# Down projection: the two sums of weight blocks per row block, made by GpSimd, are made by VectorE

## The chip, the cores and the metric

The kernel runs on one core of one Trainium2 chip. A core has a TensorE (PE in the profile: matmuls; PEld: its weight loads), a VectorE (DVE), a ScalarE (ACT), a GpSimd (POOL) and a SyncE (SP), which here only issues DMAs. Each engine works through a queue of its own, in order, and they meet at semaphores. The metric is the device time of one execution in microseconds (us). Kernel before: 2428.02 us, the median of 3 runs (2427.6 to 2429.95).

## The reference

One layer of a hybrid streaming encoder for 512 prompt frames and 64 sample frames: attention in two head groups, an output projection, and then the part this change is in, a gated feed-forward network with a residual:

```python
x = x + mix @ lp['w_out']
h = rmsnorm(x, lp['norm_ffn_g'])
x = x + (jax.nn.silu(h @ lp['ffn_w_gate']) * (h @ lp['ffn_w_up'])) @ lp['ffn_w_down']
```

The model width is 2048, the inner width of the network 5632, all in float32, so `ffn_w_down` is 5632 x 2048. A final RMSNorm closes the computation.

## The kernel before

Every product of two float32 matrices is split: an operand `w` becomes `wh`, its rounded high part (made by ScalarE, `split` at L156), and `wl`, the rest `w - wh` (made by VectorE, L153). Three matmuls, `wh*xh`, `wh*xl` and `wl*xh`, then stand for one product.

Gate, up and down projections use a seven-product scheme for 2 x 2 blocks (`winograd`). A weight tile of 256 input rows by 256 columns is taken as four 128 x 128 blocks, a11, a12, a21, a22, and the token side as two halves of 288 tokens each. Products 1, 2 and 4 take a11, a12 and a22 as they are; the others take sums, which the kernel makes on the way:

```text
product 5: s5 = a21 + a22    (GpSimd)      product 3: s3 = a12 - s6   (VectorE)
product 6: s6 = s5 - a11     (VectorE)     product 7: s7 = a11 - a21  (GpSimd)
```

Line L1192 makes all four of them. One statement picks the engine: GpSimd for products 5 and 7, VectorE for 6 and 3.

The down projection goes over the 44 input blocks of 128 in five blocks of 4 pairs and a last one of 2 pairs. For each of the first five and for each of 8 pairs of output blocks, `down_rows` runs `winograd` once; that is 40 calls, which the text below calls *row blocks*. A row block loads 1 MB of weights (`raw`, 128 x 8 x 256), and its sums are 128 x 512. For each of the seven products, in the order 1, 5, 6, 2, 7, 3, 4 (`CHAIN`), TensorE runs 8 matmuls with `wh` (L1206) and 4 with `wl` (L1210), each of 288 columns. Then VectorE adds the product from PSUM into the residual `y` (L1472). The products of a chain share PSUM banks: 1, 6, 7 and 4 use bank a, 5 and 3 bank b.

What sets the order of the work: each engine's queue is written by a scheduler, which puts an instruction where its operands and buffers allow it. Three pools of buffers matter. `wh` and `wl` have two buffers each. The sums `ws` have three (one in the first row block, where some are made in place), so that a sum takes the place of an earlier one that the split of that one has just read. `raw` has two buffers from the third row block on: the load for row block r+2 is issued on SP's queue when the last split of row block r (the `wl` of product 4) has read its tile. The operands `b` of the token side were stored to memory by the gate and up projections; those of the next block are loaded, on the same queue of SP, while the present block is computed.

The last block of 2 pairs is not done by `winograd` but by plain matmuls (`plain_rows`, L189), and the final norm and the transposes of the result close the kernel.

Of the kernel before, what the change touches and what calls it, by code (L numbers as in the profile page):

```python
# [14 lines left out]
ALU = mybir.AluOpType  # L15
# [30 lines left out]
class Streams:  # L46
# [15 lines left out]
    def take(self, name):  # L62

        free = self.slots[name]
        while not free or free[0] > self.now:
            yield max(free[0] - self.now, 0.01) if free else 0.1
        free.pop(0)
# [48 lines left out]
def encoder_step(  # L116
# [8 lines left out]
    V, S, G = nc.vector, nc.scalar, nc.gpsimd  # L125
# [29 lines left out]
    def split(hi, lo, src):  # L155
        S.activation(hi, src, AF.Copy)  # L156
        sub_lo(lo, src, hi)
# [933 lines left out]
    def pool(name, side="left"):  # L1091
        cm = tc.tile_pool(name=name, bufs=1, side=side, reuse_waits="tile")
        return cm.__enter__(), lambda: cm.__exit__(None, None, None)
# [9 lines left out]
    CHAIN = ((1, "a"), (5, "b"), (6, "a"), (2, "c"), (7, "a"), (3, "b"), (4, "a"))  # L1103
# [10 lines left out]
    def quarters(b1, b2):  # L1114
        return b1[:, 0:QH], b1[:, QH:TQ], b2[:, 0:QH], b2[:, QH:TQ]
# [35 lines left out]
    def pmt():  # L1151
        return pm.tile([P, 512], F32, name="m", tag="m")

    def winograd(wpool, spool, raws, slots, take, banks=None, engine=V, step=lambda: None, stag=("ws", 1),
                 chain=(), made=None, within=True):

        first, last = not banks, take is not None
        banks = {} if banks is None else banks

        def split_weights(n, srcs):
            wh = wpool.tile([P, n, P], F32R, name="wh", tag="wh", bufs=2)
            wl = wpool.tile([P, n, P], F32R, name="wl", tag="wl", bufs=2)
            k = 0
            for s in srcs:
                split(wh[:, k:k + s.shape[1], :], wl[:, k:k + s.shape[1], :], s)  # L1170
                k += s.shape[1]
            return wh, wl

        vs = [r.rearrange("p (m t) (f c) -> p t f m c", t=2, f=2) for r in raws]
        n = sum(v.shape[3] for v in vs)
        a11, a12, a21, a22 = ([v[:, t, f] for v in vs] for f in range(2) for t in range(2))
        sums = []

        def lhs(p):
            if made and p in made:  # L1180
                return made[p]
            if p in (5, 6, 3, 7) and (p == 5 or not within):
                w = spool.tile([P, n, P], F32, name="ws", tag=stag[0], bufs=stag[1])
                ends = np.cumsum([0] + [x.shape[1] for x in a21]).tolist()
                new = [w[:, a:b, :] for a, b in zip(ends, ends[1:])]
            else:
                new = {6: sums, 3: a12, 7: a21}.get(p)
            if p == 5:
                sums.extend(new)
            left, right = {5: (a21, a22), 6: (sums, a11), 3: (a12, sums), 7: (a11, a21)}.get(p, ((), ()))  # L1190
            for x, y, z in zip(new or (), left, right):
                (G if p in (5, 7) else V).tensor_tensor(x, y, z, op=ALU.add if p == 5 else ALU.subtract)  # L1192
            if p == 6:
                sums[:] = new
            return split_weights(n, new or {1: a11, 2: a12, 4: a22}[p])

        shared = {}
        for p, name in chain or [(p, p) for p in ORDER]:
            new = name not in shared
            if first:  # L1200
                shared[name] = banks[p] = shared[name] if not new else pmt()[:, 0:QH]
            wh, wl = lhs(p)
            for k in range(n):
                hi, lo = operands[slots[k], p]
                for x in (hi, lo):
                    PE.matmul(banks[p], wh[:, k, :], x, start=first and new and k == 0 and x is hi, stop=False,  # L1206
                              skip_group_check=not new)
            for k in range(n):
                hi, lo = operands[slots[k], p]
                PE.matmul(banks[p], wl[:, k, :], hi, start=False, stop=last and k == n - 1,  # L1210
                          skip_group_check=not new)
            if last:
                take(p, banks)
            step()
# [10 lines left out]
    ws = {}  # L1225
# [13 lines left out]
    for i in range(KC):  # L1239
        x = ma.tile([P, TQ], F32, name="x", tag="x", bufs=3)  # L1240
# [28 lines left out]
    fw, close_fw = pool("fw")  # L1269

    def load_pair(pool, src, c0, first=0):
        r = pool.tile([P, 16, 256], F32, name="raw", tag="raw", bufs=1)
        for i in range(2 - first):
# [4 lines left out]
    raw = load_pair(fr, w_gate, 0, 1)  # L1278
    banks0 = {}
    winograd(ma, ma, [raw0], range(4), None, banks0, step=lambda: next(turning, None), stag=("wr", WR_BUFS),  # L1280
             made={p: ws[2 * KC + p - 1] for p in (1, 2)})
    close_ma()
# [7 lines left out]
    def combined(c11, c12, c21, c22, chain):  # L1290

        s4 = None if chain else squad()
        s = {}
        copied = {1: c11, 5: c22, 6: c12, 4: c21}
        added = {2: (c11,), 7: (c22,) if chain is CHAIN else (c22, c21), 3: (c12,)}

        def take_sums(p, banks):
            if p in copied:
                S.activation(copied[p], banks[p], AF.Copy)
            else:  # L1300
                for c in added[p]:
                    V.tensor_tensor(c, c, banks[p], op=ALU.add)  # L1302

        if chain:
            return take_sums

        def take(p, banks):
            if p == 1:
                s[1] = s4[:, 0]
                S.activation(s[1], banks[1], AF.Copy)  # L1310
            elif p == 6:
                s[2] = s4[:, 1]
                V.tensor_tensor(s[2], s[1], banks[6], op=ALU.add)
                V.tensor_tensor(c12, s[2], banks[5], op=ALU.add)
            elif p == 3:
                V.tensor_tensor(c12, c12, banks[3], op=ALU.add)
            elif p == 7:
                V.tensor_tensor(s[2], s[2], banks[7], op=ALU.add)
                V.tensor_tensor(c22, s[2], banks[5], op=ALU.add)
                V.tensor_tensor(c21, s[2], banks[4], op=ALU.add)  # L1320
            elif p == 2:
                V.tensor_tensor(c11, s[1], banks[2], op=ALU.add)

        return take
# [47 lines left out]
    y = {}  # L1372
# [14 lines left out]
    for u in range(FC // 2):  # L1387
        out = {}
        for which, wsrc in (("g", w_gate), ("u", w_up)):
# [6 lines left out]
            chain = () if first else CHAIN if u == FC // 2 - 1 and which == "u" else WIDE  # L1396
            take = combined(*quarters(c[:, 0, :], c[:, 1, :]), chain)
# [8 lines left out]
            def step():  # L1406
                products[0] += 1
                if products[0] > (2, 1)[which == "u"]:
                    next(spilling, None)
                if u == 0 and which == "u":  # L1410
                    next(norm, None)
                if u == FC // 2 - 1 and which == "u":
                    if products[0] == 2:
                        load_y(0)
                    for _ in range(blocks[0]):
                        next(start, None)

            if first:
                winograd(fw, rw, [now], range(4, 8), take, banks0, step=step)
            else:  # L1420
                winograd(fw, rw, [now], range(8), take, step=step, chain=chain)
# [43 lines left out]
    def down_rows(m0, n, d, slots, step):  # L1465
        raws = [fetched.pop((m0, d))]
        y11, y12, y21, y22 = quarters(y[2 * d], y[2 * d + 1])
        parts = {1: (y11,), 5: (y22,), 6: (y12,), 2: (y11,), 7: (y22,), 3: (y12,), 4: (y21,)}

        def take(p, banks):  # L1470
            for c in parts[p]:
                V.tensor_tensor(c, c, banks[p], op=ALU.add)  # L1472

        spool, bufs = (yy, 3) if m0 + d else (rw, 1)
        winograd(fw, spool, raws, slots, take, step=step, stag=("ws", bufs), chain=CHAIN, within=m0 + d == 0)

    tok = [[(0, NS), (NS, P), (192, 96)], [(QH, P), (416, P), (544, 32)]]
    sqs = {}
# [72 lines left out]
    wanted, m0 = [], 0  # L1551
# [16 lines left out]
    for bi, n in enumerate(blocks):  # L1568
        slots = [(first + k) % 8 for k in range(n)]
        if bi + 1 < len(blocks):  # L1570
# [7 lines left out]
            for d in range(KC // 2):  # L1578
                if bi == 0 and d + 1 < KC // 2:
                    load_y(d + 1)  # L1580
                down_rows(first, n, d, slots, step)
                fetch_raw()
                if bi + d == 0:
                    for _ in spilling:
                        pass
                    close_rw()
                    yy, close_yy = pool("yy", "right")
# [89 lines left out]
```

## Time and profile before

| what | us |
| --- | --- |
| median of 3 runs | 2428.02 |
| the profiled execution, its own time | 2432.31 |
| its span (first to last instruction) | 2430.4 |
| TensorE busy in the span | 2379.0 |
| VectorE busy | 1895.8 |
| ScalarE busy | 1133.6 |
| GpSimd busy | 768.7 |
| the down projection's row blocks, in the span | 1892 to 2348 |

The profile is of one execution. What lies around its span is 1.9 us. It is read in groups (instructions of one line, engine and tile, with busy time and mean duration), in waits (who waited for whom, total, times, longest), and in the timeline, where each row has a start, a duration, the engine, the line, the tiles written and read, and in brackets the idle time of the engine ahead of it with what ended that. The profile shows tiles without buffer numbers, so that `wl<-ws,wh` may be the split of any of the sums.

### The profile page before, as it was taken

What the parts mean: (1) busy time and instruction counts of PE and PEld (TensorE: products, weight loads), DVE (VectorE), ACT (ScalarE), POOL (GpSimd) and SP (SyncE); (2) the same over time, 40 slices, a digit from 0 to 9 for tenths busy, and PEclk for the clock granted to TensorE, in tenths of its full rate; (3) what the DMA queues carried; (4) which work ended last, traced back from release to release, by engine and by line L of the source; (5) the groups of instructions that cost most, each with busy time, mean ns of one, the idle gap of its engine ahead of it and who ended that gap; (6) DMA issues with size and microseconds to landing.
All of it is one profiled execution on the core that took longest, in us unless ns stands there. A gap on an engine that the chain in (4) does not pass through costs nothing. (4 is left out here: it accounts for less than half of the span.)

```text
span 2430.4 us, 44051 instructions
## 1 busy us (share of the span) xinstructions
PE 2379.0 (98%) x17556; PEld 2342.8 (96%) x17556; DVE 1895.8 (78%) x2748; ACT 1133.6 (47%) x1984; POOL 768.7 (32%) x515
## 2 busy tenths in 40 slices
PE   7999999999999999999999999999999999999998
PEld 6999999989999999999999999999999999999997
DVE  5666676666665688888888888888888899888875
ACT  5455554434444554444445444444444333333355
POOL 1100000020000355465455555554554222222235
PEclk9999999999999999999999999999999999999998
DMA  8533333243333553444454445345446983663434
GB/s 226 140 94 92 85 95 91 76 142 103 104 97 109 172 153 115 153 155 134 145 163 144 138 153 163 128 144 163 146 136 210 316 280 110 228 218 107 129 105 148
DMA packets 363250, 353.02 MB, mean 145 GB/s; under 512 B 25086, under 2 KB 321684, under 8 KB 363044
## 3 DMA queue, kind: packets, MB, share of 16 engines
q1 hardware_dynamic: 361039, 344.48, 44.9%
q0 software_dynamic: 1680, 5.19, 0.7%
q8 instruction: 138, 2.26, 0.4%
q10 hardware_dynamic: 325, 0.53, 0.1%
q14 instruction: 68, 0.56, 0.1%
HBM read 271.68 MB, written 81.16 MB: 145 GB/s over the span
## 5 line engine op out<-in xcount | busy, mean ns | idle before, releaser
L1206 PE MATMUL m<-b,wh 128*128 128x288 f32 x7168 | 1046.0, 295 | 0.9 <-ACT wh L156 0.8
L1206 PEld LDWEIGHTS m<-b,wh 128*128 128x128 f32 x7168 | 982.8, 188 | 1.8 <-ACT wh L156 1.4
L1210 PE MATMUL m<-b,wl 128*128 128x288 f32 x3584 | 582.0, 297 | 6.0 <-DVE wl L153 4.4
L153 DVE TENSOR_TENSOR wl<-raw,wh 128x1024 fp32r<-128x1024 f32 (+1 forms) x379 | 530.7, 1404 | 54.1 <-ACT wh L156 53.8
L1210 PEld LDWEIGHTS m<-b,wl 128*128 128x128 f32 x3584 | 511.8, 188 | 12.3 <-DVE wl L153 11.0
L156 ACT ACTIVATE wh<-raw 128x1024 fp32r<-128x1024 f32 (+1 forms) x379 | 329.7, 874 | 379.3 <-PE m L1206 320.6
L1192 POOL TENSOR_TENSOR ws<-raw 128x512 f32<-128x512 f32 (+1 forms) x124 | 218.8, 1765 | 604.4 <-DVE wl L153 369.5
L156 ACT ACTIVATE wh<-ws 128x512 fp32r<-128x512 f32 (+1 forms) x248 | 193.4, 780 | 272.7 <-PE m L1206 97.5
L153 DVE TENSOR_TENSOR wl<-ws,wh 128x512 fp32r<-128x512 f32 (+1 forms) x248 | 246.6, 994 | 5.3 <-ACT wh L156 4.5
L108 PE MATMUL ps<-xh,wh 128*128 128x296 f32 x992 | 226.3, 310 | 0.0
L108 PE MATMUL ps<-xl,wh 128*128 128x296 f32 x992 | 218.0, 301 | 0.3 <-DVE xl L161 0.3
L108 PE MATMUL ps<-xh,wl 128*128 128x296 f32 x992 | 217.3, 300 | 0.0
L1346 DVE TENSOR_TENSOR c<-c,s 128x288 fp32r<-128x288 f32 x168 | 166.5, 991 | 0.0
L108 PEld LDWEIGHTS ps<-xh,wh 128*128 128x128 f32 x992 | 161.8, 191 | 3.5 <-issue 0.6
L108 PEld LDWEIGHTS ps<-xl,wh 128*128 128x128 f32 x992 | 162.7, 190 | 0.9 <-DVE xl L161 0.8
L108 PEld LDWEIGHTS ps<-xh,wl 128*128 128x128 f32 x992 | 162.5, 190 | 0.0
L1472 DVE TENSOR_TENSOR y<-y,m 128x288 f32<-128x288 f32 x280 | 126.0, 450 | 41.3 <-PE m L1210 41.1
L153 DVE TENSOR_TENSOR wl<-wr,wh 128x1024 fp32r<-128x1024 f32 (+1 forms) x110 | 120.7, 1097 | 31.4 <-ACT wh L156 30.0
L1192 POOL TENSOR_TENSOR raw<-raw 128x1024 f32<-128x1024 f32 (+1 forms) x46 | 141.9, 3085 | 3.5
L1302 DVE TENSOR_TENSOR c<-c,m 128x288 f32<-128x288 f32 x171 | 73.4, 450 | 88.0 <-PE m L1210 47.0
L156 ACT ACTIVATE wh<-wr 128x1024 fp32r<-128x1024 f32 (+1 forms) x110 | 102.2, 929 | 74.6 <-PE ps L108 46.3
L1365 POOL TENSOR_TENSOR c<-c,rb 128x576 f32<-128x576 f32 x44 | 78.8, 1790 | 139.0 <-ACT c L1364 139.0
(364 smaller groups left out, 3170.6 us busy)
## 6 DMA issues: line engine op xcount, KB each, us to landing
raw<-in_ffn_w_gate SPq DMA_DIRECT2D x44, 1024.0 KB, 7.3
raw<-in_ffn_w_up SPq DMA_DIRECT2D x44, 1024.0 KB, 9.2
b<-opspill SPq DMA_DIRECT2D x148, 288.0 KB, 6.0
raw<-in_ffn_w_down SPq DMA_DIRECT2D x40, 1024.0 KB, 5.6
wr<-in_w_in SPq DMA_DIRECT2D x56, 512.0 KB, 4.1
opspill<-s SPq DMA_DIRECT2D x42, 576.0 KB, 3.1
opspill<-c SPq DMA_DIRECT2D x42, 576.0 KB
wr<-in_w_out SPq DMA_DIRECT2D x16, 512.0 KB, 4.2
```

The lines of the kernel that those rows point to most:

```text
L108: self.tc.keep_in_program_order(self.pe.matmul(out, lhsT, rhs, start=start, stop=stop))
L153: V.tensor_tensor(lo, src, f32(hi), op=ALU.subtract)
L156: S.activation(hi, src, AF.Copy)
L1192: (G if p in (5, 7) else V).tensor_tensor(x, y, z, op=ALU.add if p == 5 else ALU.subtract)
L1206: PE.matmul(banks[p], wh[:, k, :], x, start=first and new and k == 0 and x is hi, stop=False, skip_group_check=not new)
L1210: PE.matmul(banks[p], wl[:, k, :], hi, start=False, stop=last and k == n - 1, skip_group_check=not new)
L1302: V.tensor_tensor(c, c, banks[p], op=ALU.add)
L1346: V.tensor_tensor(src[:, k].bitcast(F32R), src[:, k], f32(hi[:, k]), op=ALU.subtract))
L1365: G.tensor_tensor(g[:, f, :], g[:, f, :], rb2, op=ALU.mult)
L1472: V.tensor_tensor(c, c, banks[p], op=ALU.add)
```

## The change

`winograd` gets a parameter `adder` (GpSimd unless told otherwise) in the place of an unused one. It is the engine that makes the sums of products 5 and 7. The down projection hands in VectorE. The gate and up projections keep GpSimd. Nothing else is changed in the source.

```diff
-    def winograd(wpool, spool, raws, slots, take, banks=None, engine=V, step=lambda: None, stag=("ws", 1),
+    def winograd(wpool, spool, raws, slots, take, banks=None, adder=G, step=lambda: None, stag=("ws", 1),
                  chain=(), made=None, within=True):
...
             for x, y, z in zip(new or (), left, right):
-                (G if p in (5, 7) else V).tensor_tensor(x, y, z, op=ALU.add if p == 5 else ALU.subtract)
+                (adder if p in (5, 7) else V).tensor_tensor(x, y, z, op=ALU.add if p == 5 else ALU.subtract)
...
         spool, bufs = (yy, 3) if m0 + d else (rw, 1)
-        winograd(fw, spool, raws, slots, take, step=step, stag=("ws", bufs), chain=CHAIN, within=m0 + d == 0)
+        winograd(fw, spool, raws, slots, take, step=step, stag=("ws", bufs), chain=CHAIN, within=m0 + d == 0, adder=V)
```

Two sums in each of 40 row blocks, 80 instructions, go from GpSimd's queue to VectorE's. Where they land shows in VectorE's queue. The piece is from the third row block (its weights are `raw_21139`), and `raw_21282` holds the weights of the one behind it. Behind "waits", DMAHW is a DMA, Activation is ScalarE, and Pool is GpSimd. Before:

```order
L153 TENSOR_TENSOR wl_21485<-ws_21482,wh_21484 128x512 [waits Activation_49]
L1472 TENSOR_TENSOR y_21288<-y_21288,m_21460 128x288 [waits DMAHW2_49,PE_49]
L153 TENSOR_TENSOR wl_21505<-raw_21139,wh_21504 128x512 [waits Activation_49]
L1472 TENSOR_TENSOR y_21288<-y_21288,m_21440 128x288 [waits PE_49]
L153 TENSOR_TENSOR wl_21526<-ws_21523,wh_21525 128x512 [waits Activation_49]
L1192 TENSOR_TENSOR ws_21630<-ws_21609,raw_21282 128x512 [waits DMAHW0_49,DVE_49,Pool_49]
L1472 TENSOR_TENSOR y_21288<-y_21288,m_21503 128x288 [waits PE_49]
L153 TENSOR_TENSOR wl_21547<-ws_21544,wh_21546 128x512 [waits Activation_49]
L1472 TENSOR_TENSOR y_21288<-y_21288,m_21440 128x288 [waits PE_49]
L153 TENSOR_TENSOR wl_21566<-raw_21139,wh_21565 128x512 [waits Activation_49]
```

The five L153 rows are the splits for products 6, 2, 7, 3 and 4 of the third row block. The one L1192 row is s6 of the fourth. And with the change, the same stretch:

```order
L153 TENSOR_TENSOR wl_21485<-ws_21482,wh_21484 128x512 [waits Activation_49]
L1192 TENSOR_TENSOR ws_21609<-raw_21282 128x512 [waits DMAHW0_49,DVE_49]
L1472 TENSOR_TENSOR y_21288<-y_21288,m_21460 128x288 [waits DMAHW2_49,PE_49]
L153 TENSOR_TENSOR wl_21505<-raw_21139,wh_21504 128x512 [waits Activation_49]
L1472 TENSOR_TENSOR y_21288<-y_21288,m_21440 128x288 [waits PE_49]
L153 TENSOR_TENSOR wl_21526<-ws_21523,wh_21525 128x512 [waits Activation_49]
L1192 TENSOR_TENSOR ws_21630<-ws_21609,raw_21282 128x512 [waits DVE_49]
L1472 TENSOR_TENSOR y_21288<-y_21288,m_21503 128x288 [waits PE_49]
L153 TENSOR_TENSOR wl_21547<-ws_21544,wh_21546 128x512 [waits Activation_49]
L1192 TENSOR_TENSOR ws_21671<-raw_21282 128x512 [waits DVE_49]
L1472 TENSOR_TENSOR y_21288<-y_21288,m_21440 128x288 [waits PE_49]
L153 TENSOR_TENSOR wl_21566<-raw_21139,wh_21565 128x512 [waits Activation_49]
```

Two rows are new: s5 of the fourth row block (`ws_21609`), between the splits for products 6 and 2 of the third, and s7 of the fourth (`ws_21671`), ahead of the split for product 4. The wait for the DMA that brings the fourth row block's weights stood on s6, and now stands on s5, earlier in this queue by the splits for products 2 and 7 and two additions into `y`.

GpSimd's queue, before, at the same place:

```order
L1192 TENSOR_TENSOR ws_21461<-raw_21139 128x512 [waits DMAHW3_49,DVE_49]
L1192 TENSOR_TENSOR ws_21523<-raw_21139 128x512 [waits DVE_49,Pool_49]
L1192 TENSOR_TENSOR ws_21609<-raw_21282 128x512 [waits DMAHW0_49,DVE_49,Pool_49]
L1192 TENSOR_TENSOR ws_21671<-raw_21282 128x512 [waits DVE_49,Pool_49]
L1192 TENSOR_TENSOR ws_21757<-raw_21435 128x512 [waits DMAHW0_49,DVE_49,Pool_49]
```

With the change none of these rows is left there. GpSimd has no work between the gate and up projections and the last block. A last place: s5 and s7 of the first row block stand in VectorE's queue ahead of the split for product 7 of the last up projection. SP's queue keeps its rows but for two pairs of operand loads that change places.

## The prediction

> **What bounds the kernel now.** I read the windows view first, to see who is short of time in the down projection, then the waits, then the timeline of one row block. The columns of a window are its stretch, its length, and the busy time (and instructions) of PE, PEld, DVE, ACT and POOL, then the clock, the share of the DMA engines and GB/s.
>
> ```profile
> 1920.00:2340.00 420.00, 417.77 (x3107) 413.27 (x3106) 369.90 (x592) 163.41 (x260) 97.52 (x74) 1.00 0.53 177
> ```
>
> TensorE is short: it matters here only what makes it wait, and that is little. Weight loads, which show its waits best, stood still for 420 - 413.3 = 6.7 us. Next who waits, from 1904 to 2345 us:
>
> ```profile
> POOL ws L1192 <- DMA raw<-in_ffn_w_down: 211.6, 33, 8.3
> POOL ws L1192 <- DVE wl L153: 114.5, 41, 11.0
> PEld m L1210 <- DVE wl L153: 5.4, 14, 1.1
> ```
>
> TensorE waits for `wl`, VectorE's split. The first row is the one to keep in mind: GpSimd stands 33 times, 6.4 us each, until the next weights have landed. It has nothing else to do, so this costs nothing now.
>
> A row block, on VectorE's timeline. I name the L153 rows by product: the split whose end lets SP issue a load at once (2107.73 and 2118.96 below) is product 4's, and the sequence 1, 5, 6, 2, 7, 3, 4 follows from there.
>
> ```profile
> 2108.94 0.69 DVE L153 TENSOR_TENSOR wl<-ws,wh 128x512 fp32r<-128x512 f32 x1
> 2109.66 0.69 DVE L1192 TENSOR_TENSOR ws<-raw,ws 128x512 f32<-128x512 f32 x1
> 2110.27 0.45 DVE L1472 TENSOR_TENSOR y<-y,m 128x288 f32<-128x288 f32 x1
> 2110.63 0.69 DVE L153 TENSOR_TENSOR wl<-ws,wh 128x512 fp32r<-128x512 f32 x1
> 2111.75 0.46 DVE L1472 TENSOR_TENSOR y<-y,m 128x288 f32<-128x288 f32 x1 [0.44 <-PE m L1210]
> 2112.12 0.68 DVE L153 TENSOR_TENSOR wl<-raw,wh 128x512 fp32r<-128x512 f32 x1
> 2113.72 1.42 DVE L153 TENSOR_TENSOR wl<-ws,wh 128x512 fp32r<-128x512 f32 x1
> 2115.23 0.69 DVE L1192 TENSOR_TENSOR ws<-ws,raw 128x512 f32<-128x512 f32 x1
> 2115.84 0.45 DVE L1472 TENSOR_TENSOR y<-y,m 128x288 f32<-128x288 f32 x1
> 2116.20 0.69 DVE L153 TENSOR_TENSOR wl<-ws,wh 128x512 fp32r<-128x512 f32 x1
> 2116.81 0.45 DVE L1472 TENSOR_TENSOR y<-y,m 128x288 f32<-128x288 f32 x1
> 2117.17 1.71 DVE L153 TENSOR_TENSOR wl<-raw,wh 128x512 fp32r<-128x512 f32 x1
> ```
> ```profile
> 2113.30 1.29 POOL L1192 TENSOR_TENSOR ws<-raw 128x512 f32<-128x512 f32 x1 [6.18 <-DMA raw<-in_ffn_w_down]
> 2117.03 1.30 POOL L1192 TENSOR_TENSOR ws<-raw 128x512 f32<-128x512 f32 x1 [2.44 <-DVE wl L153]
> ```
> ```profile
> 2107.73 0.38 SPq L137 DMA_DIRECT2D raw<-in_ffn_w_down  x1
> 2118.96 0.38 SPq L137 DMA_DIRECT2D raw<-in_ffn_w_down  x1
> ```
> ```profile
> 2108.36 1.22 PE L1206 MATMUL m<-b,wh 128*128 128x288 f32 x8
> 2109.96 1.22 PE L1206 MATMUL m<-b,wh 128*128 128x288 f32 x8
> 2111.55 1.22 PE L1206 MATMUL m<-b,wh 128*128 128x288 f32 x8
> ```
>
> Three things stand there. A product takes TensorE 1.595 us, (2111.55 - 2108.36)/2, so a row block 7 x 1.595 = 11.17 us when nothing waits. A split takes 0.69 us alone, but 1.42 and 1.71 us where a sum of GpSimd's runs beside it. And there is a loop from load to load: load issued (2107.73), weights land, s5 (GpSimd, 2113.30), s6, the splits for products 3 and 4, next load (2118.96). How long the loop takes on average, and the loads in it:
>
> ```profile
> L137 SPq DMA_DIRECT2D raw<-in_ffn_w_down x36: 367/383/384, 1926.4 to 2324.7; - x36
> DMA to landing us min/median/max: 5.3/5.5/6.4
> ```
>
> (2324.7 - 1926.4)/35 = 11.38 us per row block, 0.21 us above TensorE's own 11.17. Over 36 row blocks TensorE loses 7.6 us.
>
> **The change part by part.**
>
> *Work.* GpSimd loses 80 sums of 1.29 us. VectorE gains 80 of 0.69 us, 55 us. What it gets back is the slowing of its splits. The columns are busy us, mean ns, idle before:
>
> ```profile
> L153 DVE TENSOR_TENSOR wl<-raw,wh 128x512 fp32r<-128x512 f32 x152 | 145.8, 966 | 15.2 <-ACT wh L156 15.1
> L153 DVE TENSOR_TENSOR wl<-ws,wh 128x512 fp32r<-128x512 f32 x156 | 129.8, 832 | 0.0
> ```
>
> Against 0.69 us this is 152 x 0.276 + 156 x 0.142 = 64 us, a part of it in the last block, where GpSimd squares `y`. So VectorE's work stays nearly what it is. Alone, without waits, a row block would cost it by start-to-start times of the rows above: addition to split 0.37 (2111.75 to 2112.12), split to addition 0.61 (2116.20 to 2116.81), split to sum 0.72 (2108.94 to 2109.66), sum to addition 0.61 (2109.66 to 2110.27). Four products have a sum, three none: 7 x 0.37 + 4 x (0.72 + 0.61) + 3 x 0.61 = 9.7 us of 11.17. By the sum of its work VectorE fits in.
>
> *Place.* It doesn't fit by order. In VectorE's new queue s5 of the next row block stands right behind the split for product 6, and it carries the wait for the load. Queued behind it are the addition of product 5, the split for product 2, and all the rest; TensorE waits for that split. Product 6's split starts at 2110.63, so VectorE would be at s5 at 2110.63 + 0.72 = 2111.35. The weights were there at about 2113.3. GpSimd stood for the load alone; now VectorE stands with all that is behind it. That closes a longer loop, and here is its price from the landing on, at the start-to-start times above:
>
> s5 0.61, addition 0.37, split 2 0.61, addition 0.37, split 7 0.72, s6 0.61, addition 0.37, split 3 0.72, s7 0.61, addition 0.37, split 4 0.69: 6.05 us, and 0.08 to SP's issue (2117.17 + 1.71 to 2118.96): 6.13 us.
>
> The same part of the old loop: s5 1.29, 0.04 to s6, then s6 0.61, 0.36, 0.61, 0.36 and the slowed split 1.71, 0.08 to the issue: 5.06 us. There the additions of products 5 and 6 and the splits for 2 and 7 went on beside GpSimd.
>
> *The load.* From issue to s5 it took 5.57 us in the row block above. The first of the 36 loads, the longest and the last:
>
> ```profile
> 1926.44 0.38 SPq L137 DMA_DIRECT2D raw<-in_ffn_w_down  x1
> ```
> ```profile
> 1932.29 1.29 POOL L1192 TENSOR_TENSOR ws<-raw 128x512 f32<-128x512 f32 x1 [6.46 <-DVE wl L153]
> ...
> 2297.29 1.29 POOL L1192 TENSOR_TENSOR ws<-raw 128x512 f32<-128x512 f32 x1 [8.27 <-DMA raw<-in_ffn_w_down]
> ...
> 2331.32 1.30 POOL L1192 TENSOR_TENSOR ws<-raw 128x512 f32<-128x512 f32 x1 [7.22 <-DMA raw<-in_ffn_w_down]
> ```
> ```profile
> 2289.64 0.37 SPq L137 DMA_DIRECT2D raw<-in_ffn_w_down  x1
> ```
> ```profile
> 2324.73 0.37 SPq L137 DMA_DIRECT2D raw<-in_ffn_w_down  x1
> ```
>
> 5.85, 7.65 and 6.59 us; over all 36, paired like this, the mean is 5.80. GpSimd takes some 0.1 us from landing (median 5.5) to start (median 5.64). How soon VectorE starts after a landing, no row shows. The bounds are 5.5 (all loads at the median, no delay) and 5.80; I take 5.70, the mean with a shorter delay, since the long loads now count in full.
>
> *Sum.* New loop 6.13 + 5.70 = 11.83 us per row block, above TensorE's 11.17 and above the 11.38 of before: 0.45 x 36 = +16.2 us. With 5.5: 11.63, +9. With 5.80: 11.93, +20. The start-to-start times are the other unknown. At their shortest in these rows (0.36, 0.60, 0.69) the chain is 5.99 with the issue; with 5.5 that is 11.49, +4. If each instruction took its whole duration (0.69, 0.45, 0.69), 6 x 0.69 + 4 x 0.45 + 0.69 = 6.63 and 0.08, with 5.70: 12.41, +37.
>
> *The start.* s5 and s7 of the first row block now stand ahead of a split of the last up projection:
>
> ```profile
> 1879.39 1.22 DVE L153 TENSOR_TENSOR wl<-raw,wh 128x1024 fp32r<-128x1024 f32 x1
> 1881.24 1.24 PE L1210 MATMUL m<-b,wl 128*128 128x288 f32 x8
> ```
>
> Its end moves from 1880.61 to about 1882.0, and its matmuls started at 1881.24: 0.8 us lost. Against it, GpSimd's two sums for the second row block slowed a split that TensorE waited for:
>
> ```profile
> 1894.34 3.18 POOL L1192 TENSOR_TENSOR ws<-raw 128x512 f32<-128x512 f32 x2
> 1896.31 1.77 DVE L153 TENSOR_TENSOR wl<-ws,wh 128x512 fp32r<-128x512 f32 x1
> 1898.13 0.80 PE L1210 MATMUL m<-b,wl 128*128 128x288 f32 x4 [1.07 <-DVE wl L153]
> ```
>
> At 0.69 the split ends 1.08 us sooner and the 1.07 go. Both together -0.3, between +0.8 and -1.1. The loads of the first four row blocks are issued early enough that s5 finds them landed. The last block keeps its order and moves as a whole.
>
> *Against the Trainium skill.* The sum on VectorE is 0.69 against 1.29 us here. The Trainium skill, GPSIMD Engine Reference, 4.1 Engine selection, puts elementwise adds on VectorE, as GpSimd is about 2x slower with two inputs; the trace agrees on the sizes, and by this rule alone the change would gain (the first rival). The Trainium skill, DVE: scalar operands, raw-bit mode, write accounting and state across instructions, 5. Flops that outlive an instruction, says that VectorE's queue is one in-order queue; that speaks against the change, since a sum that waits for a load then holds all behind it, and by this one the sum above stands.
>
> Together +16 us: the profiled execution would go from 2432.31 to 2448. The median of the runs lies 4.3 us below that execution, so 2428.02 + 16 = 2444 us.
>
> **The rivals.**
>
> 1. *The wait is hidden and the slowing of the splits goes: faster.* Then TensorE's lost 7.6 us come back, with the start 8: 2420 us. For it speak the 64 us of slowed splits and that each split has some slack ahead of its matmuls. Against it: the loop must fit 11.17 us, so the load 11.17 - 6.13 = 5.04 us, and the shortest landing is 5.3. At the shortest chain, 5.99, the load may take 5.18, still below 5.3. Chance 0.15, for a mistake of mine in the chain.
> 2. *The two cancel.* If the load counts 5.3 to 5.5 and the chain is the shortest, the loop takes 11.3 to 11.5, as before: within 5 us, 2428 us. The long loads speak against it. Chance 0.15.
> 3. *VectorE pays whole durations*, because each sum waits for the split before it to be written: 12.4 us per row block, 2465 us. The rows at 2115.84 to 2116.81 speak against it, with starts 0.36 and 0.61 apart. Chance 0.10.
>
> That the change does nothing can be left out: GpSimd's queue has none of the 80 left.
>
> **How the numbers follow.** The forecast has 0.60, own range 2432 to 2456 us (+4, the shortest chain with the load at 5.5, to +28, the load at 6.0 in the mean). A measurement of this kernel tells about 0.2%, 4.9 us, from no change. Faster 0.15 (rival 1), within 0.2% 0.15 (rival 2), slower 0.70 (forecast and rival 3). The range for 8 in 10 goes down to rival 1's time, so that half of it is in, and leaves out rival 3: 2420 to 2458 us.
>
> **What would show it.** Right: a new row in the waits, VectorE's `ws` for the DMA of `raw`, some 36 times and 50 to 80 us in all (the rest of 11.83 - 9.7 us per row block); TensorE's `wl` matmuls waiting once per row block, for the split of product 2, some 0.6 us; loads issued about 11.8 us apart; all splits in this stretch at 0.69 us; GpSimd idle from 1900 to 2350. Wrong: VectorE's wait for the load under 10 us in all, or loads 11.2 us apart (rival 1); the new wait there but loads 11.4 us apart (rival 2: the chain mis-sized); 12.4 us apart with sums that start 0.7 us or more behind the split's end (rival 3). If TensorE lost time while VectorE was neither waiting for a load nor slowed, the theory would be wrong altogether.

## The result, and the profile after

| | us | ratio to before, 95% interval |
| --- | --- | --- |
| before, median of 5 runs on the same chip | 2428.33 (2427.6 to 2429.95) | |
| after, median of 5 runs | 2437.34 (2436.73 to 2440.82) | 1.0041 (1.003 to 1.0051) |

The kernel became slower by 9.0 us. The forecast was +16, to 2444 us: the direction and the range hold, the measured loss is a bit over half of the one forecast. One of the 11 executions of the kernel with s7 alone on VectorE, below, took 3836.05 us at a granted clock of 0.557 and is left out of its median. The profiled execution of after took 2436.73 us, with a span of 2435.0 us, 4.6 us more than the span of before.

The same window as for before, with the same columns (stretch, length, busy time and instructions of PE, PEld, DVE, ACT and POOL, clock, DMA share, GB/s):

```profile
1920.00:2340.00 420.00, 411.25 (x3037) 404.25 (x3036) 348.27 (x651) 159.91 (x253) 0.00 (x0) 1.00 0.52 173
```

Weight loads of TensorE stand still for 420 - 404.25 = 15.75 us, against 6.7 before: 9.0 us more, in this stretch alone. GpSimd does nothing. VectorE is busy for 21.6 us *less* than before, with 59 more instructions: it has not become short of time. Who waits instead, from 1904 to 2355 us (engine, line, what it waited for; total, times, longest):

```profile
DVE ws L1192 <- DMA raw<-in_ffn_w_down: 44.0, 28, 2.7
PEld m L1210 <- DVE wl L153: 14.0, 23, 1.6
```

The first row is new: VectorE, not GpSimd, stands until the next weights have landed. The second is its price on TensorE, 14.0 us against 5.4. The groups, from 1900 to 2430 us (busy us, mean ns, then idle before them):

```profile
L153 DVE TENSOR_TENSOR wl<-ws,wh 128x512 fp32r<-128x512 f32 x156 | 106.6, 684 | 0.0
L153 DVE TENSOR_TENSOR wl<-raw,wh 128x512 fp32r<-128x512 f32 x149 | 105.2, 713 | 15.9 <-ACT wh L156 15.8
L1192 DVE TENSOR_TENSOR ws<-raw 128x512 f32<-128x512 f32 x78 | 53.9, 692 | 45.5 <-DMA raw<-in_ffn_w_down 44.0
```

The splits are back to 0.68 and 0.71 us in the mean (they were 0.83 and 0.97), and the 78 added sums cost 53.9 us, so the work moved as forecast. The loss shows in the timeline of one row block, VectorE's:

```profile
2110.49 0.68 DVE L153 TENSOR_TENSOR wl<-ws,wh 128x512 fp32r<-128x512 f32 x1
2112.37 0.69 DVE L1192 TENSOR_TENSOR ws<-raw 128x512 f32<-128x512 f32 x1 [1.20 <-DMA raw<-in_ffn_w_down]
2112.98 0.45 DVE L1472 TENSOR_TENSOR y<-y,m 128x288 f32<-128x288 f32 x1
2113.34 0.68 DVE L153 TENSOR_TENSOR wl<-raw,wh 128x512 fp32r<-128x512 f32 x1
2113.94 0.45 DVE L1472 TENSOR_TENSOR y<-y,m 128x288 f32<-128x288 f32 x1
2114.31 0.68 DVE L153 TENSOR_TENSOR wl<-ws,wh 128x512 fp32r<-128x512 f32 x1
2115.03 0.69 DVE L1192 TENSOR_TENSOR ws<-ws,raw 128x512 f32<-128x512 f32 x1
2115.64 0.45 DVE L1472 TENSOR_TENSOR y<-y,m 128x288 f32<-128x288 f32 x1
2116.00 0.68 DVE L153 TENSOR_TENSOR wl<-ws,wh 128x512 fp32r<-128x512 f32 x1
2116.72 0.69 DVE L1192 TENSOR_TENSOR ws<-raw 128x512 f32<-128x512 f32 x1
2117.33 0.45 DVE L1472 TENSOR_TENSOR y<-y,m 128x288 f32<-128x288 f32 x1
2117.70 0.68 DVE L153 TENSOR_TENSOR wl<-raw,wh 128x512 fp32r<-128x512 f32 x1
```

The loads that close the loop, on SP's queue:

```profile
2106.52 0.38 SPq L137 DMA_DIRECT2D raw<-in_ffn_w_down  x1
```
```profile
2118.41 0.38 SPq L137 DMA_DIRECT2D raw<-in_ffn_w_down  x1
```

The rows run from the split for product 6 (2110.49) over s5 (2112.37, the wait in brackets) to the split for product 4 (2117.70). Load to s5 took 5.85 us, s5 to the next load 6.04: 11.89 us in all. TensorE needs 11.17, and the split that comes too late for it is the one at 2113.34, queued behind s5. Its `wl` matmuls start 1.62 us behind those of the product before, where a product takes 1.595:

```profile
2112.46 0.70 PE L1210 MATMUL m<-b,wl 128*128 128x288 f32 x4
2114.08 0.80 PE L1210 MATMUL m<-b,wl 128*128 128x288 f32 x4
```

That is little, since the row block ahead of this one had been a short one, of a kind that comes below. At the same place in the second row block behind it, the weight loads stand for 0.57 us:

```profile
2137.43 0.56 PEld L1210 LDWEIGHTS m<-b,wl 128*128 128x128 f32 x4 [0.57 <-DVE wl L153]
```

The 36 loads of the loop:

```profile
L137 SPq DMA_DIRECT2D raw<-in_ffn_w_down x36: 367/383/384, 1921.9 to 2328.3; - x36
DMA to landing us min/median/max: 5.3/5.6/6.7
```

(2328.3 - 1921.9)/35 = 11.61 us apart. Before it was 11.38; the row block shown would give 11.89. So not all row blocks are alike. Read one by one, two kinds come out. In 27 of the 36, the part from s5 to the next load is 6.03 to 6.04 us. In the other 9 it is 5.07 to 5.09. One of the nine, load issued at 1992.01 and the next at 2002.81:

```profile
1996.95 0.68 DVE L153 TENSOR_TENSOR wl<-raw,wh 128x512 fp32r<-128x512 f32 x1
1997.73 0.69 DVE L1192 TENSOR_TENSOR ws<-raw 128x512 f32<-128x512 f32 x1
```

Here the split for product 2 (1996.95) stands *ahead* of s5 (1997.73). The scheduler had put s5 one product later in these nine. That takes one split and one addition out of the loop, 0.61 + 0.36 us, and the one thing that TensorE would miss is done before the wait.

### The profile page after: what moved, and what is told of

Read it like the earlier page. It is cut to its first block, busy times and chain, and to the rows that moved or that the text cites. A ratio compares the mean times of both kernels' runs of the same rounds, so it can differ in the third digit from the quotient of the medians.

```text
span 2435.0 us, 43967 instructions
## 1 busy us (share of the span) xinstructions
PE 2380.3 (98%) x17556; PEld 2342.4 (96%) x17556; DVE 1883.6 (77%) x2828; ACT 1133.2 (47%) x1984; POOL 662.7 (27%) x435
## 4 chain that ended last, share of the span: by engine, by line
PE 71%; DVE 14%; DMA 8%; ACT 3%; issue 2%; POOL 1%; SPq 0%; DVEq 0%; ACTq 0%; POOLq 0%
PE m L1206 29%; PE ps L108 18%; PE m L1210 15%; DMA raw<-in_ffn_w_down 6%; DVE wl L153 4%; DVE ws L1192 2%; PE sp L108 2%; DVE y L1472 2%; PE po L108 2%; PE m L189 1%; PE tp L112 1%; DVE b L1111 1%; ACT wh L156 1%; PE pv L108 1%; DVE e L562 1%
## 5 line engine op out<-in xcount | busy, mean ns | idle before, releaser
L1210 PE MATMUL m<-b,wl 128*128 128x288 f32 x3584 | 580.9, 297 | 10.5 <-DVE wl L153 9.8
L153 DVE TENSOR_TENSOR wl<-raw,wh 128x1024 fp32r<-128x1024 f32 (+1 forms) x379 | 491.8, 1301 | 54.4 <-ACT wh L156 54.0
L153 DVE TENSOR_TENSOR wl<-ws,wh 128x512 fp32r<-128x512 f32 (+1 forms) x248 | 223.2, 900 | 5.5 <-ACT wh L156 4.7
L1192 POOL TENSOR_TENSOR ws<-raw 128x1024 f32<-128x1024 f32 (+1 forms) x45 | 113.5, 2523 | 261.7 <-DVE wl L153 254.7
L1472 DVE TENSOR_TENSOR y<-y,m 128x288 f32<-128x288 f32 x280 | 125.5, 448 | 28.0 <-PE m L1210 27.9
L153 DVE TENSOR_TENSOR wl<-wr,wh 128x1024 fp32r<-128x1024 f32 (+1 forms) x110 | 120.6, 1096 | 31.4 <-ACT wh L156 30.1
L1192 POOL TENSOR_TENSOR raw<-raw 128x1024 f32<-128x1024 f32 (+1 forms) x45 | 141.2, 3137 | 3.4
```

Of the source, the lines that this page charges most:

```text
L153: V.tensor_tensor(lo, src, f32(hi), op=ALU.subtract)
L1192: (adder if p in (5, 7) else V).tensor_tensor(x, y, z, op=ALU.add if p == 5 else ALU.subtract)
```

## The experiments

All ratios are to the kernel before on the same chip; its median was 2426.33 us beside the first four kernels and 2424.84 us beside the last four, and differences in us are between medians. The first two pull the two moved sums apart. The theory: s5, the sum that waits for the load, costs everything, and s7 alone gains. The rival: what counts is that VectorE has more to do, whichever sum it is.

**Only s7 on VectorE** (diff against after):

```diff
-                (adder if p in (5, 7) else V).tensor_tensor(...
+                (adder if p == 7 else G if p == 5 else V).tensor_tensor(...
```

> Half of the change: s7 on VectorE, s5 stays on GpSimd. Theory (VectorE's in-order wait for the load is the cost): GpSimd stands for the load again, no VectorE wait for it; and the split for product 4 is no longer slowed by s7 beside it. The part of the loop behind the landing is 1.33 + 0.61 + 0.37 + 0.72 + 0.61 + 0.37 + 0.69 + 0.03 = 4.73 us, with a load of 5.8 this is 10.5, under TensorE's 11.15: row blocks 11.15 to 11.2 us apart, so faster than before by 6 to 8 us, about 2421. Rival (the work that VectorE gains is the cost): half the added work, half the loss, +4 to +5 us, about 2433.

Measured 2422.15 us, ratio 0.9985 (0.9976 to 0.9994): 4.2 us faster than before. Its window and its waits:

```profile
1920.00:2340.00 420.00, 417.43 (x3127) 415.35 (x3127) 347.35 (x630) 165.78 (x263) 50.80 (x37) 1.00 0.52 176
```
```profile
POOL ws L1192 <- DMA raw<-in_ffn_w_down: 243.6, 25, 10.9
...
DVE ws L1192 <- POOL ws L1192: 6.3, 5, 1.4
```

GpSimd waits for the loads again, VectorE no longer does, and TensorE's weight loads stand still for 4.65 us. The sign is the theory's, the rival's falls. The gain is a bit over half of what the theory said: the loads are still 11.29 us apart in the mean, because seven of the 36 take 6.6 to 7.6 us until s5 starts, and then s6 on VectorE waits for GpSimd's s5 (the second row), five times.

**Only s5 on VectorE** (diff against after):

```diff
-                (adder if p in (5, 7) else V).tensor_tensor(...
+                (adder if p == 5 else G if p == 7 else V).tensor_tensor(...
```

> The other half: s5 on VectorE, s7 stays on GpSimd. Theory: VectorE waits for the load in front of the split for product 2, as in the changed kernel; s7 (0.72 with its gap) leaves the loop, but the split for product 4 is slowed by GpSimd's s7 again (1.71 for 0.69): 6.43 us behind the landing, with a load of 5.75 this is 12.2 us per row block where s5 stands behind the split for product 6. In some 27 of 36 row blocks: +20 us against before, about 2448, slower than the changed kernel (2437). Rival (work): as the first half, about 2433.

Measured 2445.65 us, ratio 1.0077 (1.0065 to 1.009): 19.3 us slower than before, twice the loss of the whole change.

```profile
1920.00:2340.00 420.00, 402.07 (x2971) 394.91 (x2970) 348.87 (x601) 156.59 (x248) 45.66 (x35) 1.00 0.51 173
```
```profile
2115.14 0.69 DVE L1192 TENSOR_TENSOR ws<-raw 128x512 f32<-128x512 f32 x1 [1.89 <-DMA raw<-in_ffn_w_down]
...
2119.75 1.69 DVE L153 TENSOR_TENSOR wl<-raw,wh 128x512 fp32r<-128x512 f32 x1
```
```profile
2119.59 1.29 POOL L1192 TENSOR_TENSOR ws<-raw 128x512 f32<-128x512 f32 x1 [10.68 <-DVE wl L153]
```

VectorE's wait is there, and now the loop also holds a split of 1.69 us (2119.75), because GpSimd's s7 runs beside it (2119.59). Behind the landing this kernel takes 6.36 us where 6.43 was expected, and 32 of its 36 row blocks have the order with s5 ahead of split 2 (27 in after). The loads are 11.9 us apart. One fewer sum on VectorE made the kernel slower, so the count of sums is not what sets the time.

**The load in two halves.** If the wait for the load is the cause, weights that land sooner should remove the loss. The plan was that what s5 reads, a21 and a22, comes with a first DMA of 512 KB, and the rest with a second one. The tile is laid out by its two sets of 128 input rows (`t` below), and the second set is loaded first.

```diff
+    def load_halves(r, r0, nk, c0):
+        v = w_down[r0:r0 + nk * P, c0:c0 + 256].rearrange("(m t p) c -> p t m c", t=2, p=P)
+        for t in (1, 0):
+            load(r[:, t * nk // 2:(t + 1) * nk // 2], v[:, t])
```

> The changed kernel, with the 1 MB load of a row block issued as two of 512 KB, the half with a21 and a22 (all that s5 reads) first; the tile is laid out by halves for that. Same work on every engine. Theory: the half for s5 lands some 3.5 us after its issue instead of 5.6 (a 512 KB load in this kernel took 3.5), so the loop through s5 takes 6.04 + 3.6 = 9.6 us and no longer limits; VectorE's wait for the load falls from 44 us to under 10, row blocks 11.15 us apart, 2420 or a little less. If both halves share the DMA engines and land together, nothing changes: 2437. Rival (work of VectorE, not the wait): 2437 with the wait gone.

Measured 2449.94 us, ratio 1.0099 (1.0085 to 1.0112): 23.6 us slower than before, where about 8 faster was expected.

```profile
DVE ws L1192 <- DMA raw<-in_ffn_w_down: 60.9, 33, 4.6
PEld m L1210 <- DVE wl L153: 26.9, 27, 3.5
```
```profile
2023.56 0.69 DVE L1192 TENSOR_TENSOR ws<-raw 128x512 f32<-128x512 f32 x1 [1.77 <-DMA raw<-in_ffn_w_down]
...
2035.47 0.69 DVE L1192 TENSOR_TENSOR ws<-raw 128x512 f32<-128x512 f32 x1 [1.74 <-DMA raw<-in_ffn_w_down]
```

The edit doesn't do what was planned. A line of the kernel, which it leaves as it was, says which block is which:

```python
a11, a12, a21, a22 = ([v[:, t, f] for v in vs] for f in range(2) for t in range(2))
```

So a21 and a22 are the two row sets of one half of the columns (`f` = 1). The first DMA brings a12 and a22, the second a11 and a21, and s5 = a21 + a22 needs both. In VectorE's queue it carries both waits (DMAHW4 and DMAHW3 are two DMAs):

```text
L1192 TENSOR_TENSOR ws_21615<-raw_21285 128x512 [waits DMAHW4_49,DMAHW3_49,DVE_49]
```

The first half did land sooner than a whole load. These are the two DMAs of the row block whose s5 starts at 2023.56, issued at 2017.66 and 2018.07, each from its own issue:

```profile
L137 SPq DMA_DIRECT2D raw<-in_ffn_w_down x1: 367/367/367, 2017.7 to 2017.7; - x1
DMA to landing us min/median/max: 4.4/4.4/4.4
```
```profile
L137 SPq DMA_DIRECT2D raw<-in_ffn_w_down x1: 507/507/507, 2018.1 to 2018.1; - x1
DMA to landing us min/median/max: 5.4/5.4/5.4
```

s5 started 0.12 us after the second had landed (2018.07 + 5.37). From the first issue to s5 it took 6.34 us in the mean of the 36 row blocks, where after takes 5.85, so the loop got longer. The experiment tells nothing of the case it was made for. That case, halves by columns, was not run. If its first half landed after 4.4 us too, the loop would take 4.4 + 0.1 + 6.04 = 10.5 us, under TensorE's 11.17; that is an estimate from the rows shown here.

**The same halves in the kernel before.**

> The kernel before (both sums on GpSimd), with the load in the same two halves. It tells what GpSimd's slowing of the splits costs by itself, once the load is early. Theory: the loop was 5.06 us behind the landing and limited only with loads above 6.1; GpSimd's s5 now runs earlier, so most of the 7.6 us that TensorE loses go away: 2421 to 2424. If the slowed splits cost TensorE by themselves, it stays at 2427 to 2428, and the difference to the changed kernel with halves is the gain of moving the sums.

Measured 2435.57 us, ratio 1.0033 (1.002 to 1.0045), 9.2 us slower than before, where a gain was expected. GpSimd's s5 reads both halves as well: from the first issue to s5 it took 6.20 us in the mean, where before takes 5.80. The lateness reaches VectorE and TensorE:

```profile
DVE ws L1192 <- POOL ws L1192: 29.1, 22, 2.1
PEld m L1210 <- DVE wl L153: 14.2, 36, 0.9
```

It is no test of an early load either. It agrees with a loop in which a later load costs time in either kernel, but does not show it, since the number of DMAs changed too.

**s5 two products later in VectorE's queue.** The work of after stays on VectorE, all four sums. Only the buffers of the sums are shared in another way: s5 and s7 share one buffer, s6 and s3 two. Then the next s5 can be made when the split for product 7 has read s7, and the scheduler puts it there, two products later, when the load has long landed.

```diff
-                w = spool.tile([P, n, P], F32, name="ws", tag=stag[0], bufs=stag[1])
+                w = spool.tile([P, n, P], F32, name="ws",
+                    **(dict(tag="wx", bufs=2) if p in own else dict(tag=stag[0], bufs=stag[1])))
...
-        spool, bufs = (yy, 3) if m0 + d else (rw, 1)
+        spool, bufs = (yy, 1) if m0 + d else (rw, 1)
+        ... own=(6, 3) if m0 + d else (), ...
```

(At the kernel's end, the tiles of the result take turns in the same three buffers.)

> The changed kernel with the same three buffers for sums, shared out otherwise: one for s5 and s7, two for s6 and s3. The scheduler then puts s5 of the next row block behind the split for product 7, two products later, where it can take the place of s7; all work stays on VectorE. Theory (the place of the waiting sum in VectorE's queue is the cost): behind the landing come s5 0.61, addition 0.37, split 3 0.72, s6 0.61, addition 0.37, split 4 0.69, 0.03 to the issue = 3.40 us, with a load of 5.75 this is 9.2, under TensorE's 11.15: row blocks 11.15 us apart, the wait for the load under 15 us in all, faster than before by 6 to 9 us, about 2420. Rival (work of VectorE): like the changed kernel, +9 us.

Measured 2416.9 us, ratio 0.9966 (0.9954 to 0.9979): 7.9 us faster than before and the fastest that does the whole computation.

```profile
1920.00:2340.00 420.00, 420.00 (x3165) 420.00 (x3165) 360.23 (x674) 168.56 (x268) 1.19 (x1) 1.00 0.53 177
```
```profile
2106.16 0.69 DVE L153 TENSOR_TENSOR wl<-ws,wh 128x512 fp32r<-128x512 f32 x1
2106.88 0.69 DVE L1192 TENSOR_TENSOR ws<-raw 128x512 f32<-128x512 f32 x1
```

TensorE never stands still in the window. s5 (2106.88) now comes behind the split for product 7 (2106.16) and waits for nothing: it starts 7.90 us after the issue of its load, issued at 2098.98, and the loads are 11.15 us apart, TensorE's own pace (11.17 by the rows that the forecast read).

**The same sharing, but s5 where it was.** A control for the buffers and for the result's tiles: s7 goes to the other two buffers as well, so that s5 has one to itself.

(The diff is against the experiment before this one.)

```diff
-        ... own=(6, 3) if m0 + d else (), ...
+        ... own=(6, 3, 7) if m0 + d else (), ...
```

> The control to that: again one buffer and two, but the one for s5 alone and the two for s6, s7 and s3. s5 stays behind the split for product 6 in 31 of 36 row blocks (27 in the changed kernel), and s3 stands in the loop in the place of s7: 6.05 us again. Theory: 11.8 us per row block there, +9 to +12 us against before, like the changed kernel or a little slower. If the way the buffers are shared out, or the output tiles that share them at the end, made the difference, this one would be as fast as the other.

Measured 2432.4 us, ratio 1.0029 (1.0018 to 1.0041), 7.6 us slower than before; 9 to 12 were expected.

```profile
1920.00:2340.00 420.00, 413.26 (x3050) 405.69 (x3049) 345.84 (x654) 157.27 (x254) 0.00 (x0) 1.00 0.52 174
```
```profile
DVE ws L1192 <- DMA raw<-in_ffn_w_down: 41.1, 30, 3.9
```

The wait and most of the loss are back. So what gained in the experiment before this was the place of s5, not the sharing. Behind the landing it takes 5.91 us instead of 6.04. The control isn't the changed kernel in all: s6 comes later in its queue, and 6.4 of the 14.3 us that TensorE's weight loads stand still are waits for ScalarE's `wh`, of which there were none in after.

**After and before without the loads.** The last question is whether anything but the load costs time: VectorE's 55 us of added work in after, the splits slowed by GpSimd in before.

```diff
+            if len(key) == 2 and len(kept) == 2:
+                fetched[key] = kept[(key[0] // 4 * 8 + key[1]) % 2]
+                return
...
+            if len(kept) < 2:
+                kept.append(fetched[key])
```

> The changed kernel without the loads of the row blocks from the fifth on: they read the weights of the third and fourth again (35 MB less are read and the result is another one, the work on every engine is the same). Theory: no wait for a load, row blocks 11.15 us apart, 8 us under before: 2419 to 2421. The rest that is then left is what VectorE's gained work costs; rival (work): about 2435.

> The kernel before, without the same loads. What TensorE still loses is the price of GpSimd's sums beside VectorE's splits alone. Theory: splits stay slowed (1.4 to 1.7 us beside a sum), but have slack: row blocks 11.15 to 11.2 us apart, 2420 to 2423. If the slowing costs by itself, 11.3 to 11.4 and 2426 to 2428.

After without loads: 2417.47 us, ratio 0.9969 (0.9957 to 0.998), 7.4 us faster than before. Before without loads: 2420.4 us, ratio 0.998 (0.9971 to 0.9989), 4.4 us faster. Their windows, in this order:

```profile
1920.00:2340.00 420.00, 420.00 (x3166) 420.00 (x3165) 366.01 (x672) 169.43 (x270) 3.91 (x4) 1.00 0.24 83
```
```profile
1920.00:2340.00 420.00, 420.00 (x3165) 420.00 (x3164) 360.24 (x601) 168.00 (x265) 94.40 (x73) 1.00 0.25 86
```

TensorE is busy throughout in both. In after without loads, s5 stands right behind the split for product 6 in every row block of this window, and with nothing to wait for it costs nothing there. So VectorE's sums cost TensorE nothing in the row blocks, and neither do the splits that GpSimd slows in the other kernel (it is busy for 94.40 us, and the splits from `raw` take 1.02 us in the mean instead of 0.69). All that before lost there, and all that after loses there, hangs on the loads. This doesn't make slowed splits free: in the row block of before that the forecast read, the splits for products 7 and 4 (1.42 and 1.71 us) lie between s5 and the next load, in the loop.

The readings together, from the windows 1920 to 2340 (weight loads standing still: 420 less their busy time) and the differences of the medians:

| kernel | still, us | against before | time against before, us |
| --- | --- | --- | --- |
| before | 6.7 | | |
| after | 15.75 | +9.0 | +9.0 |
| only s7 on VectorE | 4.65 | -2.1 | -4.2 |
| only s5 on VectorE | 25.1 | +18.4 | +19.3 |
| after, load in halves | 29.0 | +22.3 | +23.6 |
| before, load in halves | 14.2 | +7.5 | +9.2 |
| s5 two products later | 0.0 | -6.7 | -7.9 |
| control | 14.3 | +7.6 | +7.6 |
| after without loads | 0.0 | -6.7 | -7.4 |
| before without loads | 0.0 | -6.7 | -4.4 |

The one stretch accounts for each time within 2.3 us. A third `raw` buffer, which would let each load start a row block sooner, wasn't tried: three buffers take 24 KB of each partition, and 18.1 are left for them.

## Why the prediction was right in direction and too large

*What bounds, and what the change does to it.* Borne out. The loop from load to load sets the pace as soon as it is longer than TensorE's 11.17 us; VectorE waits for the load in order; TensorE misses the split queued behind s5. Taking the wait away (s5 two products later) or the load (no loads) turns the loss into a gain of 7 to 8 us; that is what the first rival had priced, 2420 us. Its condition, a hidden wait, wasn't met by this change.

*Work.* Right: splits at 0.68 and 0.71, 53.9 us of sums, no bound by VectorE's total.

*The part behind the landing.* 6.13 us was forecast, 6.04 measured where the order is the one of the piece that the forecast read. The start-to-start times of before (0.37, 0.61, 0.72) hold within 0.01 us in the rows of after quoted above, wherever VectorE doesn't wait; the third rival, whole durations, falls with them. The 5.06 us that the forecast gave for the same part of the old loop is not what its row block shows: from s5 (2113.30) to the next load (2118.96) there are 5.66 us, because s6 stood behind the slowed split for product 7. Only behind the two latest loads is it 5.04 and 5.05. The sum didn't use this figure.

*The load.* 5.70 was taken; the mean over 36 is 5.85, and 5.83 in the 27 row blocks. With 6.04 that is 11.87 there, against 11.83 forecast: two errors that nearly cancel, which is luck. The line of landings (5.3/5.5/6.4 in before) holds only the 16 of the 36 loads whose landing is recorded, and not the one of 7.65 us.

*The sum: the step that failed.* "Over 36 row blocks" was wrong: "+0.45 x 36" took the order of one piece of VectorE's queue for all. By what was measured, 27 x (11.87 - 11.38) - 9 x (11.38 - 10.98) = +13.2 - 3.6 = +9.6 us in place of +16.2; from the loads' mean distance directly, 36 x (11.645 - 11.387) = +9.3. The nine row blocks, where s5 stands behind split 2, took 10.98 us each in the mean, less than before. They stand in VectorE's queue as it was written before any run, and could have been read there row block by row block.

*The start.* -0.3 was forecast, between +0.8 and -1.1. The stretch ahead of the first row blocks, before and then after:

```profile
1890.00:1900.00 10.00, 8.44 (x62) 7.97 (x61) 7.59 (x9) 4.05 (x9) 5.82 (x4) 1.00 1.07 382
```
```profile
1890.00:1900.00 10.00, 9.99 (x76) 9.78 (x75) 9.68 (x18) 5.32 (x11) 1.97 (x1) 1.00 1.07 378
```

TensorE's weight loads got 1.8 us back, more than the bound of 1.1. Two stalls of before went, 0.7 us for ScalarE's `wh` and 1.3 for VectorE's `wl`, where only the second had been counted, with 1.07 us. In before without loads this stretch is as it was in before (7.68 us busy), in after without loads as in after (9.78): that explains 2.1 of the 3 us between those two kernels. And the 0.8 us that the sums of the first row block were to cost TensorE at the last up projection did not come. VectorE there, and TensorE:

```profile
1877.42 0.69 DVE L1192 TENSOR_TENSOR ws<-raw 128x512 f32<-128x512 f32 x1
1878.15 0.69 DVE L1192 TENSOR_TENSOR raw<-raw 128x512 f32<-128x512 f32 x1
1878.76 1.22 DVE L153 TENSOR_TENSOR wl<-raw,wh 128x1024 fp32r<-128x1024 f32 x1
```
```profile
1879.21 1.24 PE L1210 MATMUL m<-b,wl 128*128 128x288 f32 x8
...
1882.40 1.24 PE L1210 MATMUL m<-b,wl 128*128 128x288 f32 x8
```

The two sums stand ahead of the split, as the forecast said. But the split ends at 1879.98, after the `wl` matmuls of 1879.21 had begun, so these can't be its own: the next are those of 1882.40, with 2.4 us to spare. The pair that the forecast read, a split and the `wl` matmuls of 1881.24, is the same one in before (both traces have 16 and 8 matmuls in turn, 3.19 us apart): it gave the split the matmuls of one product too early.

*The signs.* VectorE's wait came 28 times and 44.0 us, where "some 36 times and 50 to 80 us" was said: the nine row blocks again, and VectorE also spends 27.9 us waiting for TensorE. TensorE's waits for splits came 23 times, where once per row block was said; their size, 14.0/23 = 0.61 us each, is as said. Loads 11.61 apart, not 11.8. GpSimd idle, as said.

*What stays open.* In the spans the account closes: -2.3 ahead of the changed place, -2.3 from there to the first load of the loop, +9.3 in the loop, -0.1 behind it, makes +4.6. The medians differ by 9.0 (7.3 to 12.4 by the interval). The first load of the down projection, ahead of everything the change touches, was issued at 1866.57 us in the one execution and at 1864.30 in the other; these 2.3 us of scatter belong to the two executions alone. Without them the account is +6.9, a little under the lower end of the interval, and the other 2.1 us up to the medians aren't explained. Nor is it shown why the scheduler wrote nine row blocks in the other order.

*Two rules beside the traces.* The Trainium skill, GPSIMD Engine Reference, 4.1 Engine selection, puts an elementwise add on VectorE; 0.69 against 1.29 us agrees. With s7 the rule gained 4.2 us, with s5 it lost 19.3 us: it is about durations, and here the place in the queue decided. The Trainium skill, SBUF — State Buffer, Who interferes with whom, says that a VectorE operation with two inputs in SBUF contends with a GpSimd operation that reads SBUF. The traces agree in that splits beside a sum took 1.42 to 1.71 us in the rows shown, instead of 0.69; but in before without loads TensorE lost nothing by it in the row blocks.

## What to carry to other kernels

As s5 did on VectorE here, an instruction that waits for a DMA holds what is queued behind it on its engine: give it to an engine with nothing else to do, or put it so late that the data has landed. To judge such a move, add up the loop from a load's issue over landing and last reader back to the next issue, with start-to-start times, compare it with the pace of the engine that is short, and read the order in all repetitions, not in one. When a load is split so that a reader can start sooner, look up in the source which part each operand of the reader is in. Which buffers share a slot can decide that order: with the same sums on the same engine it made the difference between 9.0 us lost and 7.9 us gained.

## What the runs showed of the hardware that was not expected

Two DMAs of 512 KB, issued 0.4 us apart on one queue, landed one after the other. In the kernel with halves both landings are recorded for nine row blocks. In all nine the first half landed 4.3 to 5.3 us after its issue, and the second 1.4 to 2.5 us after the first. Together they were no sooner there than one load of 1 MB: 5.7 to 7.8 us from the first issue, against 5.3 to 6.7 from the issue in after.

Where it waits for nothing, VectorE mostly starts an addition from PSUM 0.60 to 0.61 us after the start of an operation of 0.69 us, and the next split 0.36 to 0.37 us after the start of an addition of 0.45 us (the medians of every kernel here). A sum of durations would count not quite a tenth of a microsecond too much each time.

Splits beside a sum of GpSimd's were slow in before and cost TensorE nothing once the loads were out of the way: in before without loads the splits from `raw` still take 1.02 us in the mean, and TensorE is busy for all of the 420 us.
